# Last norm moved behind the next output, weight sums moved to VectorE, and gate staging regrouped in a one-core encoder block

## The chip, the cores and the metric

The kernel runs on one core of a Trainium2 chip. The metric is the device time of one execution in microseconds (us). The core's engines are named as the profile names them: PE (TensorE matmul) and PEld (its weight loads), DVE (VectorE), ACT (ScalarE), POOL (GpSimd) and SP (SyncE, which here only issues DMAs). Each engine works through its own queue in order and waits on semaphores set by the others.

## The reference

One layer over 16 meta tokens and 1024 frames of width 1024, all in float32:

```python
h = concat([meta, x])                                # 1040 x 1024
xn = rms_norm(h, g0);  proj = xn @ w_in              # q, k, v, forget gate, two output gates
o_a = forgetting_attention(q_a, k_a, v_a, log_f)     # 8 heads of 64
o_b = stick_breaking_attention(q_b, k_b, v_b)        # 8 heads of 64
mixed = (sigmoid(g_a) * (o_a @ w_o_fox) + sigmoid(g_b) * (o_b @ w_o_sb)) @ w_out
h = h + rms_norm(mixed, g1)
u = causal_depthwise_conv(rms_norm(h, g2) @ w_up, conv_w, conv_b)   # 3 taps, 2 x 2816 channels
u_gate, u_val = split(u, 2)
ffn = (gelu(u_gate) * u_val) @ w_down                # 2816 -> 1024
h = h + rms_norm(ffn, g3);  return h[:, 16:]
```

## The kernel before

Features lie on the 128 partitions and tokens along the free axis. Every float32 product is made from two halves, a rounded high part and a rest ("hi" and "lo", of type fp32r): weight hi times input hi, weight hi times input lo, weight lo times input hi. A weight block is loaded into a raw buffer (`load_w`, tag `wraw`, three buffers), ACT casts the high half, and another engine subtracts it for the low half.

The order of instructions on each engine is not written out. A scheduler goes through the program with a timeline simulation of its own and puts instructions that are ready on the engines by priority, which is program order unless `tc.high_priority` lifts it. A tile with a `tag` takes one of the tag's `bufs` buffers and waits until the tile that held it has been read for the last time.

The stages in order:

- Heads. Sixteen heads of attention, with the projections and the gate products (`gate(x)`, 16 of them; the last seven come after the heads in program order) as further work for PE. A gate product is made in three token pieces (`PCS`: 246, 390 and 390 columns after the first 14 are dropped), scaled on DVE into a staging tile `gst` (L485) and stored to memory `gd` (L486). The tag `gst` has two buffers for all three pieces.
- Output projection (L567 on). For each of eight feature blocks `o`, `load_w(wo[o])` with the low half subtracted on POOL, the products `y`, and the gates, loaded again from `gd`.
- Merge and up-projection of the first value and gate blocks as plain products (`plain_tile`), interleaved with the second norm. Their results `us` (value and gate half in one tile) are stored to `ud` for a later convolution.
- Strassen stage. `strassen(lf, js, nxt)` makes one pair of up-projection blocks (gate, value) from seven products instead of eight for each of the token blocks `js`. `Left` prepares the left operands of the following pair in four parts: `first` loads the weights and forms the four sums s1 to s4 (L760 to L763, on POOL, 128x512 each, into `sA` and `sB`), `second`, `third` and `fourth` cast and split. The seven products end in copies on ACT (`keep`, L793 and L824) and adds on DVE (L797), both lifted by priority. At its end `conv_gate` does the convolution of value and then gate (`c`: one ACT instruction L720, two on DVE L722 each), GELU on ACT (L725), their product on DVE (L726), and the store to `gdr`. In six of the pairs `late_conv` does the same for a `us` stored before. The tile `c` has two buffers for the gate and one for the value.
- Down-projection. The 512-token blocks t = 0 and t = 1 are taken one after the other. `hidden(t, k)` loads a block of the hidden layer again (tag `graw`, three buffers) and splits it. `down(t, [o])` makes output block `o` from 22 inputs in pieces of 8, 7 and 7 (`CK`), 66 matmuls of 512 columns, with weights through `wraw`; then ACT squares the result (`fs`, L935), DVE sums the squares (`sas`, L936), and ACT stores the scaled result in `acc` (L937). `last_norm(t, c0, c1)` forms the norm (L133 on: two small groups of matmuls, a square root on ACT, and DVE in between), multiplies `acc` by it (L950), adds the residual `hr` loaded from `hd` (L951; `hr` takes `wraw` buffers) and stores the output (L952). For t = 1 the weights of the last two output blocks are kept (`kept`, loads named `wr_k`, all twelve after output 2), because these outputs are made in two halves of 256 tokens at the end, where the first half's norm runs beside the second half's products.

The lines at the end of the down-projection that set the order:

```python
        last_norm(0, 0, NB)
        for o in range(KT - 2):
            down(1, [o])
            if o == 2:
                ...
        for c0 in (0, 256):
            for o in (KT - 2, KT - 1):
                down(1, [o], c0, c0 + 256, kept)
                if c0 and o == KT - 2:
                    last_norm(1, 0, 256)
        last_norm(1, 256, NB)
```

Of the kernel before, what the change touches and what calls it, by code (L numbers as in the profile page):

```python
# [8 lines left out]
F32 = mybir.dt.float32  # L9
# [40 lines left out]
def block_kernel(ctx, tc, xa, xb, wqk, wv, wf, bfg, wg, wo, wout, wup, wdn, gains, conv, cst, out):  # L50
# [114 lines left out]
    with ExitStack() as pa:  # L165
# [309 lines left out]
        def gate(x):  # L475
            i = x // 2 + 8 * (x % 2)
            hi, lo = load_w(wg[i], KT * P, f"g{i}")
            for k, (n0, n1) in enumerate(PCS):
                m0 = max(n0, A0)
                w = n1 - m0  # L480
                ps = pl.tile([P, 512], F32, tag="lin", name=f"pg{i}{k}")
                products(ps[:, :w], hi, lo, xs[k], 0, KT, m0 - n0, n1 - n0)
                st = xp.tile([P, 390], F32, tag="gst", bufs=2, name=f"gst{i}{k}")
                with tc.high_priority(offset=200):
                    nc.vector.tensor_tensor(st[:, :w], ps[:, :w], rs1[:, m0:n1], op=ALU.mult)  # L485
                nc.sync.dma_start(gd[i][:, m0 - A0 : n1 - A0], st[:, :w])  # L486

# [49 lines left out]
    with ExitStack() as pb1:  # L537
# [29 lines left out]
        for o in range(KT):  # L567
            hi, lo = load_w(wo[o], KT * P, f"o{o}")
            if o > 1:
# [131 lines left out]
    def plain_tile(k, j, s, us, eng=None):  # L701

        wt = load_w(wup[2 * k + s], KT * P, f"u{k}{j}{s}", eng or nc.vector)
        r = right[j]
        for c in range(2):
            ps = bank(f"pu{k}{j}{s}{c}")
            mm3(ps, wt, [r[f"b{kh + 1}{c + 1}"] for kh in range(2)])
            nc.scalar.copy(us[:, s, c, :], ps)

    def u_tile(k, j):  # L710
        return cvp.tile([P, 2, 2, QW], F32, tag="us", bufs=2, name=f"us{k}{j}")

    def conv_gate(k, j, us):
        cv = []
        for s in (1, 0):
            x = 2 * k + s
            c = cvp.tile([P, 2, 256], F32, tag=f"c{s}", bufs=2 - s, name=f"c{x}{j}")
            cv.append(c)
            u = us[:, s]
            nc.scalar.activation(c, u[:, :, 2:QW], AF.Identity, bias=cb[:, x, 3:4], scale=cb[:, x, 2:3])  # L720
            for tap in (1, 0):
                nc.vector.scalar_tensor_tensor(c, u[:, :, tap : tap + 256], cb[:, x, tap : tap + 1], c,  # L722
                                               op0=ALU.mult, op1=ALU.add)
        v, g = cv
        nc.scalar.activation(g, g, AF.Gelu_apprx_tanh)  # L725
        nc.vector.tensor_tensor(g, g, v, op=ALU.mult)  # L726
        nc.sync.dma_start(gdr[k][:, j * NB : (j + 1) * NB], g.rearrange("p h t -> p (h t)"))

    def late_conv(k):
        us = u_tile(k, 0)  # L730
        nc.sync.dma_start(us, ud[k])
        conv_gate(k, 0, us)

    class Left:
# [13 lines left out]
        def first(self):  # L748
# [10 lines left out]
            s2, s4, s3, s1 = self.sA[:, 0:512], self.sA[:, 512:1024], self.sB[:, 0:512], self.sB[:, 512:1024]  # L759
            nc.gpsimd.tensor_tensor(s1, a21, self.a22, op=ALU.add)  # L760
            nc.gpsimd.tensor_tensor(s2, s1, a11, op=ALU.subtract)
            nc.gpsimd.tensor_tensor(s4, a12, s2, op=ALU.subtract)
            nc.gpsimd.tensor_tensor(s3, a11, a21, op=ALU.subtract)  # L763

# [9 lines left out]
    def strassen(lf, js, nxt, kept_order=None):  # L774
# [27 lines left out]
        for j in js:  # L802
            r = psR.tile([P, 512], F32, tag="R", name=f"R{k}{j}")[:, :QW]
            product("a12", "b21", j, r, True)
            add(us[j][:, 0, 0, :], r, kept["p1", j])
        if nxt:
# [8 lines left out]
        for j in js:  # L815
            product("s1", "t1", j, A[j])
            keep(j, "v")
            add(us[j][:, 1, 1, :], B[j], kept["v", j])
        if nxt:
            nxt.second()  # L820
        for j in js:
            product("s4", "b22", j, A[j])
            with tc.high_priority(offset=400):
                nc.scalar.copy(us[j][:, 0, 1, :], A[j])  # L824
        if nxt:
            nxt.third()
        for j in js:
            product("a22", "t4", j, B[j])
            add(us[j][:, 1, 0, :], B[j], kept["u2", j])
        if nxt:  # L830
            nxt.fourth()
        for j in js:
            conv_gate(k, j, us[j])

# [6 lines left out]
    for x in range(2 * NPL):  # L841
        k, s = x // 2, x % 2
        if s == 0:
            us = u_tile(k, 0)
        plain_tile(k, 0, s, us)
        if s:
            nc.sync.dma_start(ud[k], us)
        go(2 if x in (0, 1, 2, 3) else 1)
# [51 lines left out]
    with ExitStack() as pd:  # L900
# [15 lines left out]
        def down(t, os, c0=0, c1=NB, kept=None):  # L916

            w = c1 - c0
            if os[0] == 0:
                sas.append(dpb.tile([P, NB], F32, tag="sas", name=f"sas{t}"))  # L920
            pss = [psD.tile([P, 512], F32, tag="dn", name=f"pd{t}{o}{c0}")[:, :w] for o in os]
# [8 lines left out]
            for o, ps in zip(os, pss):  # L930
                if o == 0:
                    nc.scalar.activation(sa, ps, AF.Square)
                else:
                    s2 = dpb.tile([P, 512], F32, tag="fs", name=f"fs{t}{o}{c0}")[:, :w]
                    nc.scalar.activation(s2, ps, AF.Square)  # L935
# [3 lines left out]
        def last_norm(t, c0, c1):  # L939
# [4 lines left out]
            for o in range(0, KT, st):  # L944
                hr = wp.tile([P, st, w], F32, tag="wraw", bufs=3, name=f"hr{t}{c0}{o}")
                for c in range(c0, c1, 256):
                    nc.sync.dma_start(hr[:, :, c - c0 : c - c0 + 256], hd[2 * t + c // 256][:, o : o + st, :])
                for q in range(0, st, 2):
                    a = acc[:, o + q : o + q + 2, :]
                    nc.vector.tensor_tensor(a, a, rs.to_broadcast([P, 2, w]), op=ALU.mult)  # L950
                    (nc.gpsimd if o < 4 else nc.vector).tensor_tensor(a, a, hr[:, q : q + 2, :], op=ALU.add)  # L951
                    (nc.sync if q else nc.scalar).dma_start(  # L952
                        out[o + q : o + q + 2, :, t * NB + c0 : t * NB + c1].rearrange("k p t -> p k t"), a)
# [9 lines left out]
        for k in range(11, NK):  # L963
            hidden(1, k)
        last_norm(0, 0, NB)
        kept = {KT - 2: [], KT - 1: []}
        KC = [(k, min(k + 4, NK)) for k in range(0, NK, 4)]
        for o in range(KT - 2):
            down(1, [o])
            if o == 2:  # L970
                end = None
                n = 0
                for j, (k0, k1) in enumerate(KC):
                    for x in kept:
                        c = (k1 - k0) * P
                        if c == 512 or end is None:
                            end = slot(dpa if n < 5 else dpb, f"k{n}")
                            n += 1
                            wt = [e[:, :c] for e in end]
                        else:  # L980
                            wt = [e[:, c : 2 * c] for e in end]
                        if c == 512:
                            end = None
                        load_w(wdn[x][:, k0 * P : k1 * P], c, f"k{x}{j}", nc.vector, wt)
                        kept[x].append(wt)
        for c0 in (0, 256):
# [76 lines left out]
```

## Time and profile before

| What | Value |
|---|---|
| Median of 3 runs | 1746.5 us (1746.47 to 1746.73) |
| The profiled execution's own time | 1743.7 us |
| Its span in the trace | 1741.7 us |
| PE busy | 1652.4 us, 95% of the span |
| DVE busy | 1145.1 us, 66% |
| ACT busy | 821.5 us, 47% |
| POOL busy | 578.3 us, 33% |

The span is the time between the first and the last instruction of the profiled execution; the execution's own time lies around it. In the windows of the profile each engine has its busy us and, in brackets, the number of its instructions, in the order PE, PEld, DVE, ACT, POOL, followed by the granted clock of PE (1.00 is full), the share of DMA time and GB/s. A timeline's row gives start, duration, engine, line, operation and tiles, and in brackets at the end what the engine waited for. In a row of grouped instructions the last bar is followed by the idle time ahead of them and its releaser.

### The profile page before, as it was taken

What the parts mean: (1) busy time and instruction counts of PE and PEld (TensorE: products, weight loads), DVE (VectorE), ACT (ScalarE), POOL (GpSimd) and SP (SyncE); (2) the same over time, 40 slices, a digit from 0 to 9 for tenths busy, and PEclk for the clock granted to TensorE, in tenths of its full rate; (3) what the DMA queues carried; (4) which work ended last, traced back from release to release, by engine and by line L of the source; (5) the groups of instructions that cost most, each with busy time, mean ns of one, the idle gap of its engine ahead of it and who ended that gap; (6) DMA issues with size and microseconds to landing.
All of it is one profiled execution on the core that took longest, in us unless ns stands there. A gap on an engine that the chain in (4) does not pass through costs nothing.

```text
span 1741.7 us, 29748 instructions
## 1 busy us (share of the span) xinstructions
PE 1652.4 (95%) x11592; PEld 1586.6 (91%) x11592; DVE 1145.1 (66%) x1881; ACT 821.5 (47%) x1702; POOL 578.3 (33%) x402
## 2 busy tenths in 40 slices
PE   7999999999989899989999999998999999996897
PEld 7899999999989899989999999998999998884687
DVE  8656566665879887745436885999887877333322
ACT  4345445544556565444345554555454556332321
POOL 3456556565445564314302013222232300001001
PEclk9999999999999899999999999999999999997899
DMA  4222221211111012265343542333213238444421
GB/s 166 71 64 63 63 61 59 61 57 52 38 43 41 27 50 63 63 189 159 96 146 125 180 148 71 110 110 116 97 68 103 68 130 251 134 141 149 144 81 61
DMA packets 78237, 170.59 MB, mean 98 GB/s; under 512 B 10224, under 2 KB 37360, under 8 KB 78096
## 3 DMA queue, kind: packets, MB, share of 16 engines
q1 hardware_dynamic: 75920, 165.54, 30.5%
q10 hardware_dynamic: 2176, 3.15, 0.5%
q8 instruction: 91, 1.49, 0.4%
q14 instruction: 50, 0.41, 0.1%
HBM read 126.43 MB, written 35.77 MB: 93 GB/s over the span
## 4 chain that ended last, share of the span: by engine, by line
PE 73%; DVE 12%; DMA 6%; ACT 4%; issue 3%; POOL 0%; DVEq 0%; SPq 0%; ACTq 0%; POOLq 0%
PE pd L913 12%; PE pg L118 9%; PE pq L118 9%; PE A L786 7%; PE pm L611 5%; PE y L118 5%; PE pv L118 5%; PE pu L611 4%; DVE c L722 4%; PE po L431 4%; PE B L786 3%; PE tr L421 3%; PE R L786 2%; PE s L349 2%; PE s L348 2%
## 5 line engine op out<-in xcount | busy, mean ns | idle before, releaser
L913 PE MATMUL pd<-g,wh_d 128*128 128x512 f32 x616 | 194.8, 397 | 23.4 <-ACT wh_d L106 21.9
L722 DVE SCALAR_TENSOR_TENSOR c<-us,cb,c 128x512 f32<-128x512 f32 x176 | 161.6, 932 | 21.5 <-ACT c L720 20.1
L913 PEld LDWEIGHTS pd<-g,wh_d 128*128 128x128 f32 x616 | 117.3, 191 | 51.8 <-ACT wh_d L106 23.9
L393 POOL TENSOR_SCALAR pr<-pr,mx 128x144 f32<-128x144 f32 (+3 forms) x64 | 114.9, 1801 | 102.6 <-DVE mx L392 63.5
L913 PE MATMUL pd<-g,wl_d 128*128 128x512 f32 x308 | 122.4, 397 | 0.4 <-DVE wl_d L92 0.3
L426 DVE TENSOR_TENSOR pt<-tr,pt 128x512 fp32r<-128x512 f32 (+1 forms) x160 | 98.2, 632 | 36.9 <-ACT pt L425 34.3
L401 POOL TENSOR_TENSOR pr<-pr,kp 128x143 f32<-128x143 f32 (+3 forms) x64 | 80.5, 1258 | 121.6 <-DVE kp L398 69.6
L951 POOL TENSOR_TENSOR acc<-acc,hr 128x512 f32<-128x512 f32 (+1 forms) x6 | 9.7, 1639 | 332.7 <-DVE acc L950 332.7
L92 DVE TENSOR_TENSOR wl_d<-wr_d,wh_d 128x896 fp32r<-128x896 f32 (+1 forms) x42 | 47.7, 1137 | 109.8 <-ACT wh_d L106 108.6
L760 POOL TENSOR_TENSOR sB<-wu 128x512 f32<-128x512 f32 x20 | 26.3, 1317 | 279.2 <-DVE s3wlo L92 196.1
L431 PE MATMUL po<-pt,vv 128*128 128x256 f32 (+1 forms) x640 | 110.1, 282 | 7.7 <-DVE pt L426 5.9
L431 PEld LDWEIGHTS po<-pt,vv 128*128 128x128 f32 x640 | 94.6, 190 | 9.7 <-DVE pt L426 6.8
L425 ACT CAST pt<-tr 128x512 fp32r<-128x512 f32 (+1 forms) x160 | 83.0, 545 | 35.6 <-PE tr L421 33.9
L106 ACT CAST wh_d<-wr_d 128x896 fp32r<-128x896 f32 (+1 forms) x42 | 41.1, 979 | 121.2 <-PE pd L913 100.4
L720 ACT ACTIVATE c<-us,cb 128x512 f32<-128x512 f32 x88 | 71.2, 816 | 52.3 <-DVE c L726 23.6
L386 ACT ACTIVATE pr<-s,mx 128x144 f32<-128x144 f32 (+6 forms) x112 | 59.8, 540 | 75.9 <-DVE mx L384 60.3
L421 PE MATMUL tr<-cs,pr 128*128 128x128 f32 x576 | 91.2, 275 | 0.0
L398 DVE TENSOR_TENSOR_SCAN kp<-kp 128x16 f32<-128x16 f32 (+3 forms) x64 | 89.1, 1394 | 0.4
L118 PE MATMUL pg<-xh,wh_g 128*128 128x390 f32 (+1 forms) x384 | 76.0, 331 | 4.9 <-DVE gst L485 4.9
L348 PE MATMUL s<-k,q 128*128 128x264 f32 (+9 forms) x240 | 80.1, 338 | 0.0
L118 PE MATMUL pq<-xl,wh_qk 128*128 128x390 f32 (+1 forms) x384 | 78.7, 329 | 0.0
L118 PE MATMUL pq<-xh,wh_qk 128*128 128x390 f32 (+1 forms) x384 | 77.7, 329 | 0.0
(288 smaller groups left out, 4745.8 us busy)
## 6 DMA issues: line engine op xcount, KB each, us to landing
wu<-in_wup SPq DMA_DIRECT2D x40, 512.0 KB
wr_d<-in_wdn SPq DMA_DIRECT2D x28, 448.0 KB
gdr<-c SPq DMA_DIRECT2D x44, 256.0 KB
gr<-gdr SPq DMA_DIRECT2D x44, 256.0 KB
gs<-gd SPq DMA_DIRECT2D x16, 513.0 KB
wr_qk<-in_wqk SPq DMA_DIRECT2D x16, 512.0 KB
wr_g<-in_wg SPq DMA_DIRECT2D x16, 512.0 KB
wr_wo<-in_wout SPq DMA_DIRECT2D x16, 512.0 KB
```

The lines of the kernel that those rows point to most:

```text
L118: marks["mm"] = nc.tensor.matmul(ps, w[:, k * P : (k + 1) * P], x[:, k - k0, n0:n1], start=(k == k0 and s == 0), stop=(k == k1 - 1 and s = ...
L348: nc.tensor.matmul(ps[:tn, :n], q2[:, t0 : t0 + tn], k1[:, s0:s1], start=True, stop=False)
L393: nc.gpsimd.tensor_scalar(pr[:, :w], pr[:, :w], z, None, op0=ALU.mult)
L398: nc.vector.tensor_tensor_scan(r, r, r, kp[:, w - P : w - P + 1], op0=ALU.mult, op1=ALU.bypass)
L421: nc.tensor.transpose(tr[:, x * P : (x + 1) * P], prs[tb][:, NM + j * P : NM + (j + 1) * P], ident)
L425: nc.scalar.copy(pt[:, 0, :n], tr[:, :n])
L426: nc.vector.tensor_tensor(pt[:, 1, :n], tr[:, :n], f(pt[:, 0, :n]), op=ALU.subtract)
L431: nc.tensor.matmul(po[:, o0:256], vj, pt[:, s, 256 * j : min(256 * j + 256, n)], start=False, stop=(last and j == 1 and s == 1))
L611: nc.tensor.matmul(ps, (hi, hi, lo)[s][:, c : c + P], xs[kh][s == 1][:, k, :], start=(s == 0 and kh == 0 and k == 0), stop=(s == 2 and kh ...
L722: nc.vector.scalar_tensor_tensor(c, u[:, :, tap : tap + 256], cb[:, x, tap : tap + 1], c, op0=ALU.mult, op1=ALU.add)
L786: nc.tensor.matmul(ps, w[:, (k0 + i) * P : (k0 + i + 1) * P], x[:, i, :], start=(first and s == 0 and i == 0), stop=(s == 2 and i == 3), s ...
L913: nc.tensor.matmul(ps, a[:, (k - k0) * P : (k - k0 + 1) * P], x[:, c0:c1], start=(k == 0 and s == 0), stop=(k == NK - 1 and s == 2))
```

## The change

- Gate staging: pieces 0 and 1 go to one tile of 636 columns with one store, piece 2 to a tile of 390 columns; each tile has its own tag and one buffer.
- Output projection: the low halves of `wo` are subtracted on DVE.
- `us` becomes two tiles, one for each half; `ud` is stored and loaded in two parts. The convolution of a half is a function of its own, `half_conv`. In `strassen` the gate half is convolved ahead of the last product (a22 with t4); in the other places the gate comes first and then the value.
- The sums s1 to s4 are made on DVE.
- The norm of block 0 comes after output 0 of block 1. Its residual tiles are eight tiles of 512 columns with tag `graw`, each loaded in two parts, and all its adds are on DVE. The squares `fs` take `graw` buffers too, and `sas` has a buffer for each block. Of the stores of `out` only one kind stays on the ACT queue (second half of block 1, even pairs); the others go through SP.
- The kept weights are loaded two at a time after each of block 1's first six outputs.

```diff
@@ gate
-                st = xp.tile([P, 390], F32, tag="gst", bufs=2, name=f"gst{i}{k}")
+                if k != 1:
+                    st = xp.tile([P, PCS[1][1] - A0 if k == 0 else L - PCS[1][1]], F32, tag=f"gst{k}", name=f"gst{i}{k}")
+                    a0 = m0
                 with tc.high_priority(offset=200):
-                    nc.vector.tensor_tensor(st[:, :w], ps[:, :w], rs1[:, m0:n1], op=ALU.mult)
-                nc.sync.dma_start(gd[i][:, m0 - A0 : n1 - A0], st[:, :w])
+                    nc.vector.tensor_tensor(st[:, m0 - a0 : n1 - a0], ps[:, :w], rs1[:, m0:n1], op=ALU.mult)
+                if k:
+                    nc.sync.dma_start(gd[i][:, a0 - A0 : n1 - A0], st)
@@ output projection
-            hi, lo = load_w(wo[o], KT * P, f"o{o}")
+            hi, lo = load_w(wo[o], KT * P, f"o{o}", nc.vector)
@@ us, conv_gate
-        return cvp.tile([P, 2, 2, QW], F32, tag="us", bufs=2, name=f"us{k}{j}")
...
+        return [cvp.tile([P, 2, QW], F32, tag=f"us{s}", bufs=2, name=f"us{s}{k}{j}") for s in range(2)]
+
+    def half_conv(k, j, s, u):
+        x = 2 * k + s
+        c = cvp.tile([P, 2, 256], F32, tag=f"c{s}", bufs=2 - s, name=f"c{x}{j}")
+        nc.scalar.activation(c, u[:, :, 2:QW], AF.Identity, bias=cb[:, x, 3:4], scale=cb[:, x, 2:3])
+        for tap in (1, 0):
+            nc.vector.scalar_tensor_tensor(c, u[:, :, tap : tap + 256], cb[:, x, tap : tap + 1], c,
+                                           op0=ALU.mult, op1=ALU.add)
+        if s == 0:
+            nc.scalar.activation(c, c, AF.Gelu_apprx_tanh)
+        return c
+
+    def conv_gate(k, j, us, g=None):
+        g = half_conv(k, j, 0, us[0]) if g is None else g
+        v = half_conv(k, j, 1, us[1])
         nc.vector.tensor_tensor(g, g, v, op=ALU.mult)
         nc.sync.dma_start(gdr[k][:, j * NB : (j + 1) * NB], g.rearrange("p h t -> p (h t)"))
@@ late_conv
-        nc.sync.dma_start(us, ud[k])
+        for s in range(2):
+            nc.sync.dma_start(us[s], ud[k][:, s])
@@ Left.first
-            nc.gpsimd.tensor_tensor(s1, a21, self.a22, op=ALU.add)
-            nc.gpsimd.tensor_tensor(s2, s1, a11, op=ALU.subtract)
-            nc.gpsimd.tensor_tensor(s4, a12, s2, op=ALU.subtract)
-            nc.gpsimd.tensor_tensor(s3, a11, a21, op=ALU.subtract)
+            nc.vector.tensor_tensor(s1, a21, self.a22, op=ALU.add)
+            nc.vector.tensor_tensor(s2, s1, a11, op=ALU.subtract)
+            nc.vector.tensor_tensor(s4, a12, s2, op=ALU.subtract)
+            nc.vector.tensor_tensor(s3, a11, a21, op=ALU.subtract)
@@ strassen
         if nxt:
             nxt.third()
+        gs = {j: half_conv(k, j, 0, us[j][0]) for j in js}
         for j in js:
             product("a22", "t4", j, B[j])
-            add(us[j][:, 1, 0, :], B[j], kept["u2", j])
+            add(us[j][1][:, 0, :], B[j], kept["u2", j])
         if nxt:
             nxt.fourth()
         for j in js:
-            conv_gate(k, j, us[j])
+            conv_gate(k, j, us[j], gs[j])
@@ down
-                    s2 = dpb.tile([P, 512], F32, tag="fs", name=f"fs{t}{o}{c0}")[:, :w]
+                    s2 = dpa.tile([P, 512], F32, tag="graw", bufs=3, name=f"fs{t}{o}{c0}")[:, :w]
@@ last_norm
-                hr = wp.tile([P, st, w], F32, tag="wraw", bufs=3, name=f"hr{t}{c0}{o}")
-                for c in range(c0, c1, 256):
-                    nc.sync.dma_start(hr[:, :, c - c0 : c - c0 + 256], hd[2 * t + c // 256][:, o : o + st, :])
+                if w == NB:
+                    hr = [dpa.tile([P, NB], F32, tag="graw", bufs=3, name=f"hr{t}{o + i}") for i in range(st)]
+                else:
+                    hr = wp.tile([P, st, w], F32, tag="wraw", bufs=3, name=f"hr{t}{c0}{o}")
+                    nc.sync.dma_start(hr, hd[2 * t + c0 // 256][:, o : o + st, :])
                 for q in range(0, st, 2):
                     a = acc[:, o + q : o + q + 2, :]
                     nc.vector.tensor_tensor(a, a, rs.to_broadcast([P, 2, w]), op=ALU.mult)
-                    (nc.gpsimd if o < 4 else nc.vector).tensor_tensor(a, a, hr[:, q : q + 2, :], op=ALU.add)
-                    (nc.sync if q else nc.scalar).dma_start(
+                    if w == NB:
+                        for i in range(2):
+                            for c in range(2):
+                                nc.sync.dma_start(hr[i][:, 256 * c : 256 * (c + 1)], hd[2 * t + c][:, o + i, :])
+                            nc.vector.tensor_tensor(a[:, i, :], a[:, i, :], hr[i], op=ALU.add)
+                    else:
+                        (nc.gpsimd if o < 4 else nc.vector).tensor_tensor(a, a, hr[:, q : q + 2, :], op=ALU.add)
+                    (nc.scalar if c1 == NB and c0 and not q else nc.sync).dma_start(
                         out[o + q : o + q + 2, :, t * NB + c0 : t * NB + c1].rearrange("k p t -> p k t"), a)
@@ order of the down-projection
-        last_norm(0, 0, NB)
...
+        def keep_w(j, x):
...
+            load_w(wdn[x][:, k0 * P : k1 * P], c, f"k{x}{j}", nc.vector, wt)
+            kept[x].append(wt)
+
         for o in range(KT - 2):
             down(1, [o])
-            if o == 2:
...
+            if o == 0:
+                last_norm(0, 0, NB)
+            for x in kept:
+                keep_w(o, x)
```

More of the change, by code (lines that the diff above doesn't have):

```diff
@@ L707, in plain_tile @@
             mm3(ps, wt, [r[f"b{kh + 1}{c + 1}"] for kh in range(2)])
-            nc.scalar.copy(us[:, s, c, :], ps)
+            nc.scalar.copy(us[s][:, c, :], ps)
     def u_tile(k, j):
-        return cvp.tile([P, 2, 2, QW], F32, tag="us", bufs=2, name=f"us{k}{j}")
[L713 to L725, printed above, removed]
+        return [cvp.tile([P, 2, QW], F32, tag=f"us{s}", bufs=2, name=f"us{s}{k}{j}") for s in range(2)]
[12 more added lines that the diff above has]
+        v = half_conv(k, j, 1, us[1])
         nc.vector.tensor_tensor(g, g, v, op=ALU.mult)
@@ L804, in strassen @@
             product("a12", "b21", j, r, True)
-            add(us[j][:, 0, 0, :], r, kept["p1", j])
+            add(us[j][0][:, 0, :], r, kept["p1", j])
         if nxt:
@@ L817, in strassen @@
             keep(j, "v")
-            add(us[j][:, 1, 1, :], B[j], kept["v", j])
+            add(us[j][1][:, 1, :], B[j], kept["v", j])
         if nxt:
@@ L823, in strassen @@
             with tc.high_priority(offset=400):
-                nc.scalar.copy(us[j][:, 0, 1, :], A[j])
+                nc.scalar.copy(us[j][0][:, 1, :], A[j])
         if nxt:
             nxt.third()
+        gs = {j: half_conv(k, j, 0, us[j][0]) for j in js}
         for j in js:
             product("a22", "t4", j, B[j])
-            add(us[j][:, 1, 0, :], B[j], kept["u2", j])
+            add(us[j][1][:, 0, :], B[j], kept["u2", j])
         if nxt:
@@ L846, in block_kernel @@
         if s:
-            nc.sync.dma_start(ud[k], us)
+            for u in range(2):
+                nc.sync.dma_start(ud[k][:, u], us[u])
         go(2 if x in (0, 1, 2, 3) else 1)
@@ L919, in down @@
             if os[0] == 0:
-                sas.append(dpb.tile([P, NB], F32, tag="sas", name=f"sas{t}"))
+                sas.append(dpb.tile([P, NB], F32, name=f"sas{t}"))
             pss = [psD.tile([P, 512], F32, tag="dn", name=f"pd{t}{o}{c0}")[:, :w] for o in os]
@@ L964, in block_kernel @@
             hidden(1, k)
-        last_norm(0, 0, NB)
         kept = {KT - 2: [], KT - 1: []}
         KC = [(k, min(k + 4, NK)) for k in range(0, NK, 4)]
+        end = None
+        def keep_w(j, x):
+            nonlocal end
+            k0, k1 = KC[j]
+            c = (k1 - k0) * P
+            if c == 512 or end is None:
+                n = 2 * j + x % 2
+                end = slot(dpa if n < 5 else dpb, f"k{n}")
+                wt = [e[:, :c] for e in end]
+            else:
+                wt = [e[:, c : 2 * c] for e in end]
+            if c == 512:
+                end = None
+            load_w(wdn[x][:, k0 * P : k1 * P], c, f"k{x}{j}", nc.vector, wt)
+            kept[x].append(wt)
         for o in range(KT - 2):
             down(1, [o])
-            if o == 2:
[L971 to L985, printed above, removed]
+            if o == 0:
+                last_norm(0, 0, NB)
+            for x in kept:
+                keep_w(o, x)
         for c0 in (0, 256):
```

## The prediction

> **What bounds the kernel now.** I read the page's busy table first, then the windows stage by stage, then the waits of PE, and at each wait the chain or the timelines.
>
> ```profile
> span 1741.7 us, 29748 instructions
> PE 1652.4 (95%) x11592; PEld 1586.6 (91%) x11592; DVE 1145.1 (66%) x1881; ACT 821.5 (47%) x1702; POOL 578.3 (33%) x402
> 1100.00:1200.00 100.00, 94.43 (x771) 93.18 (x772) 93.96 (x116) 58.03 (x98) 29.91 (x20) 1.00 0.31 100
> 1200.00:1400.00 200.00, 191.53 (x1562) 188.93 (x1561) 164.75 (x201) 103.38 (x177) 64.64 (x44) 1.00 0.27 90
> 1500.00:1550.00 50.00, 50.00 (x221) 41.09 (x220) 13.14 (x15) 13.46 (x18) 0.00 (x0) 1.00 0.33 96
> 1573.74:1593.43 19.69, 3.12 (x10) 1.47 (x11) 10.00 (x10) 3.77 (x5) 4.66 (x2) 0.56 0.43 141
> 1573.74:1693.50 119.76, 95.01 (x392) 75.11 (x392) 40.49 (x43) 32.41 (x44) 4.66 (x2) 0.87 0.42 131
> ```
>
> PE (the first busy column of a window; then PEld, DVE, ACT, POOL, granted clock) is the bound nearly everywhere, so the change can win only where PE stands still. Three places belong to it. The Strassen stage (1100 to 1400) loses 5.57 + 8.47 = 14.0 us of PE, with DVE at 94% in its first third. The hole after 1573.74 leaves PE 16.6 us without work. And the second block's first six outputs of the down-projection, 1573.74 to 1693.50, are 6 x 66 = 396 matmuls that take 119.76 us; at the undisturbed pace of the 1500 to 1550 row, 50.00 / 221 = 0.2262 us each, they are 89.6 us.
>
> ```profile
> PE A L786 <- ACT v L793: 4.7, 4, 1.4
> PE A L786 <- DVE a11wlo L92: 3.3, 4, 1.1
> PE B L786 <- ACT s3whi L743: 2.8, 4, 0.7
> PE B L786 <- DVE us L797: 2.5, 2, 1.9
> PE pd L913 <- ACT wh_d L106: 21.9, 2, 13.8
> ```
>
> PE's waits of the two stages (total, times, longest): 13.3 us in the Strassen stage, all on ACT or DVE work that comes late; 21.9 us in the down-projection, two holes. Their chain and the SP timeline:
>
> ```profile
> 1577.51 2.09 PE rr_d L148 x2
> 1584.24 2.58 DVE acc L951
> 1586.84 5.48 DMA out<-acc
> 1592.33 1.05 ACT wh_d L106
> 1565.88 18.44 SPq L947 DMA_DIRECT2D hr<-hd  x4
> 1586.84 31.57 SPq L99 DMA_DIRECT2D wr_d<-in_wdn  x9
> 1623.18 19.70 SPq L99 DMA_DIRECT2D wr_k<-in_wdn  x12
> 1644.14 31.02 SPq L99 DMA_DIRECT2D wr_d<-in_wdn  x9
> ```
>
> First hole: the last norm of block 0 stands ahead of block 1's weights. Its residual tiles `hr` hold the three `wraw` buffers; the first weight load goes out at 1586.84, when the add that reads `hr` ends (1584.24 + 2.58), and PE restarts one load and one cast later. The chain calls that load a store, but the SP row shows `wr_d` issued at that moment. Second hole: twelve loads `wr_k` occupy the same three buffers from 1623.18 and the next `wr_d` waits until 1644.14.
>
> **The change, term by term.** (1) Last norm and kept weights. `hr` moves from `wraw` to `graw`, so no weight load waits for it. The norm comes after block 1's first output, so while it runs three pieces of weights are in or on their way. The kept loads go two per output instead of twelve in a row. Both holes lose their cause. What remains in place: the norm's own matmuls, and DVE work that stands in front of weight splits.
>
> ```profile
> 1721.13 0.50 PE L138 MATMUL rp_d<-cs,sas 128*128 128x1 f32 x4
> 1725.26 0.59 PE L148 MATMUL rr_d<-dg_d,one_sq 128*128 128x256 f32 x2
> L950 DVE TENSOR_TENSOR acc<-acc,rr_d 128x1024 f32<-128x1024 f32 x4 | 4.6, 1217 | 2.2 <-PE rr_d L148 2.2
> L726 DVE TENSOR_TENSOR c<-c,c 128x512 f32<-128x512 f32 x6 | 4.1, 685 | 0.0
> 1593.43:1603.43 10.00, 9.96 (x36) 7.58 (x37) 3.39 (x3) 1.88 (x2) 0.00 (x0) 0.83 0.62 226
> 1649.09:1659.09 10.00, 9.96 (x31) 7.49 (x32) 2.79 (x3) 1.88 (x2) 0.00 (x0) 0.72 0.33 115
> ```
>
> The matmuls cost PE 0.50 plus twice 0.59 for the double width, 1.5 us with rounding. DVE gets four multiplications (4.6 us) and, now all on it, eight adds of 512 columns at 0.69 (the L726 row has that shape): 10.1 us. A weight piece keeps PE busy 24 x 0.2262 = 5.4 us, and its successor's cast and split need 1.05 + 1.23 (the chain's 1.05, and 1.2 as in the multiplication's row), so some 3 us of slack per piece meets single instructions of 0.7 to 1.2 us. Where an add waits for its `hr`, the split queued behind it on DVE waits too; SP has sixteen `hr` loads of 128 KB instead of eight of 256 KB, and the four stores move from the ACT queue to SP, where each waits for an add and holds whatever is behind it. I put 1.5 us on that, between 0 (all within the slack) and 13.7 (priced as a rival below). The extra 2 x 256 KB per output lie under 15 us of matmuls. The squares that now share `graw` hold a buffer only until DVE has added them; an output's PSUM has four banks, so a late square delays no matmul by itself. Sum: 119.76 - 89.6 - 1.5 - 1.5 = 27.2 us saved. About 5 us of it is the slow clock after each hole, not the holes: 36 and 31 matmuls in 10 us where 44 fit.
>
> (2) Strassen stage. Four sums per weight block move from POOL to DVE, 80 in all.
>
> ```profile
> L722 DVE SCALAR_TENSOR_TENSOR c<-us,cb,c 128x512 f32<-128x512 f32 x176 | 161.6, 932 | 21.5 <-ACT c L720 20.1
> L722 DVE SCALAR_TENSOR_TENSOR c<-us,cb,c 128x512 f32<-128x512 f32 x22 | 16.4, 748 | 2.0 <-ACT c L720 2.0
> L92 DVE TENSOR_TENSOR a22ul<-wu,a22uh 128x512 fp32r<-128x512 f32 x19 | 29.1, 1534 | 0.0
> L92 DVE TENSOR_TENSOR a22ul<-wu,a22uh 128x512 fp32r<-128x512 f32 x1 | 0.7, 690 | 0.0
> L760 POOL TENSOR_TENSOR sB<-wu 128x512 f32<-128x512 f32 x16 | 21.1, 1318 | 174.7 <-DVE s3wlo L92 174.7
> 1146.51 3.42 DVE L722 SCALAR_TENSOR_TENSOR c<-us,cb,c 128x512 f32<-128x512 f32 x2
> 1146.33 1.32 POOL L760 TENSOR_TENSOR sB<-wu 128x512 f32<-128x512 f32 x1 [13.89 <-DVE s3wlo L92]
> 1147.61 1.77 POOL L763 TENSOR_TENSOR sB<-wu,wu 128x512 f32<-128x512 f32 x1
> 1143.22 1.05 ACT L743 CAST s3whi<-sB 128x1024 fp32r<-128x1024 f32 x1
> 1164.75 1.05 ACT L743 CAST s3whi<-sB 128x1024 fp32r<-128x1024 f32 x1
> ```
>
> The same DVE instruction takes 748 ns in the window 1400 to 1450, where POOL has nothing, and 932 on average over the stage; a22ul takes 690 alone and 1534 in the stage. In the timeline two L722 that stand beside POOL's sums take 3.42 us together. So POOL's sums already cost DVE 176 x 0.184 + 19 x 0.844 = 48 us. On DVE itself the 80 sums are 80 x 0.69 = 55 us. DVE's load thus stays as it is, within 7 us over 350 us. What changes is lateness: a 1.7 us stall in front of an urgent add goes, and a 0.69 us sum that has some 15 us until its cast (L763 writes sB until 1149.38, and its cast runs at 1164.75) comes instead. The gate half, convolved before the last product and gate first in the late blocks, lets its GELU on ACT follow two DVE steps instead of four, which is where "A <- ACT v" comes from: the copy that frees bank A is queued on ACT behind a GELU that waits for DVE. The split `us` adds six loads and six stores on SP, hidden as the old ones were. I take the 2.5 us of "us" fully and half of the 10.8 us of the other three waits: 2.5 + 5.4 = 7.9 us saved. Bounds: all 13.3; and below nothing, 9 us lost, if the L722 stay as slow as they are and the sums come on top in the six blocks with late convolutions: one takes 21.5 us (1143.22 to 1164.75) and 0.94 x 21.5 = 20.2 of DVE; with 4 x 0.69 more that is 23.0, 1.5 longer, six times.
>
> The Trainium skill, "SBUF — State Buffer", section "Who interferes with whom", says a DVE instruction with two SBUF inputs and a GpSimd instruction that reads SBUF exclude each other for the whole instruction. The rows agree that both get longer, but not that all of POOL's time is lost to DVE. By that rule of the Trainium skill the return would be POOL's whole busy time in the stage, 29.9 + 64.6 = 95 us of 1100 to 1400, and the 55 us of sums would be more than paid; by the rows it is the 48 us above.
>
> (3) Gate staging and output projection. The two stores per gate replace three; pieces 0 and 1 share one buffer, so the next gate's first product waits for a store issued after piece 1 rather than for one two pieces back. In the head loop these stores have tens of us. In the last gates they have not:
>
> ```profile
> 744.00:784.00 40.00, 33.98 (x218) 33.37 (x217) 20.12 (x40) 17.04 (x37) 8.38 (x5) 0.91 0.76 207
> PE pg L118 <- DVE gst L485: 4.9, 1, 4.9
> 762.49 1.01 SPq L486 DMA_DIRECT2D gd<-gst  x2
> ```
>
> Both stores left only at 762.49, behind loads on SP; with one store of 318 KB in the place of the two the wait lasts about as long. I take 0, between 6.0 us gained (all of PE's idle time in that window) and 5 lost (the wait once more, for the larger store). The eight low halves of `wo` cost DVE 1.2 us each instead of POOL's time, beside a DVE that is half idle: 0; without that cover 8 x 1.2 = 10 us.
>
> (4) Tail: block 1's first half stores all go through SP, so ACT no longer issues a store ahead of its last square:
>
> ```profile
> 1729.83 0.38 ACTq L952
> ```
>
> 0.4 us saved, all of this row, since SP has nothing else there that the end waits for.
>
> Sum: 27.2 + 7.9 + 0 + 0.4 = 35.5 us. The profiled execution took 1743.7 us (span 1741.7), so 1708.2; the median of the runs shown lies 2.8 above it: 1711.
>
> **The rivals.** A. The Strassen stage gives nothing back, since DVE's load is unchanged and other late instructions replace those: 27.6 us saved, 1719. Against it stands that POOL's sums now hit urgent instructions at random.
> B. The first hole moves rather than goes: the norm's eight `hr` tiles pass three `graw` buffers in three rounds of 5.5 us (the load at 1586.84), with 10.1 us of DVE in order, 26.6 us, under one output's cover of 66 x 0.2262 = 14.9 us; 11.7 us exposed plus 2 of slow clock, 13.7. In the place of the 1.5 allowed, of term 1 then 15.0 remain, with the rest 23.3: 1723.
> C. DVE is freed by the whole of POOL's busy time and all 13.3 us come back, and the gate stage gains a little: 27.2 + 13.3 + 0.4 and up to 6.0, 41 to 47 saved, 1700 to 1706. The 932 against 748 speaks for less. (By the rule of the Trainium skill's SBUF page named above it would come out so.)
> D. Slower than before: DVE becomes the bound of the Strassen stage. If L722 is slow for another reason than POOL and each sum takes as long as a22ul does there (1.53), 80 sums add 122 us to a DVE that has only 41 us of room in 1100 to 1400 (300 - 93.96 - 164.75): some 80 us lost against 27.6 saved, 1799. It decides against the change above (41 + 27) / 80 = 0.86 us per sum with L722 unchanged. The 690 and 748 rows, both with POOL idle, speak against it.
> E. The change doesn't do what it says: a scheduled order that again puts `wr_d` behind the norm's work and the kept loads. Then only term 2 is left, or nothing: about 1739 to 1746.
>
> **How the numbers follow.** My forecast 0.55, A 0.20, B 0.09, C 0.09, D 0.04, E 0.03. Changes below about 0.2% (3.5 us) can hardly be told from none here; the forecast and A to C are all beyond that, and E is split. Faster 0.94, same 0.02, slower 0.04. The range reaches from 1701, inside C, to 1726, just above B.
>
> **What would show it.** Term 1: no PE wait on `wh_d` over 2 us after the first block's end, a granted clock of 1.00 through it, and 396 matmuls in about 93 us. Term 2: POOL empty in the Strassen stage, L722 at about 750 ns throughout, DVE's busy share there within a few per cent of before, and PE's waits there near 5 us. Term 3: PE's idle time of 744 to 784 still near 6 us. The forecast falls if the waits on `wh_d` come back behind `hr` or behind the stores on SP, if L722 stays near 930, or if PE waits in the Strassen stage for sums queued on DVE.

## The result, and the profile after

| | Time, us | Ratio to before, 95% interval |
|---|---|---|
| Before | 1746.5 | |
| Changed | 1705.6 | 0.9764 (0.9745 to 0.9783) |
| Changed, measured a second time | 1706.0 | 0.9765 (0.9752 to 0.9778) |

The change saves 41 us where 35.5 were forecast; 1705.6 lies inside the range of 1701 to 1726. One of the changed kernel's four executions took 3219.85 us and one of the ten of experiment e3 2019.0; the medians count them, the ratios leave them out.

The page of the changed kernel, its busy table:

```profile
span 1704.2 us, 29666 instructions
PE 1648.1 (97%) x11592; PEld 1585.0 (93%) x11592; DVE 1139.8 (67%) x1975; ACT 821.0 (48%) x1702; POOL 440.1 (26%) x312
```

PE has lost 4 us of busy time and 33 us of idle time; DVE has 94 instructions more and is busy 5 us less. To see where the time came from, the span is cut at two moments that exist in every trace: the first Strassen product, and the first matmul `pd` of the down-projection. The stage between them in the kernel before, in the changed one and, for later use, with the sums alone (e2) and without the early gate half (e10):

```profile
1043.51:1450.17 406.66, 392.62 (x3219) 388.56 (x3217) 333.04 (x420) 221.61 (x378) 110.73 (x76) 1.00 0.31 103
1044.32:1437.99 393.67, 390.67 (x3219) 389.14 (x3217) 323.36 (x495) 223.29 (x378) 0.00 (x0) 1.00 0.31 104
1045.97:1435.74 389.77, 388.09 (x3218) 387.26 (x3217) 323.66 (x495) 223.07 (x378) 0.00 (x0) 1.00 0.32 105
1043.25:1433.11 389.86, 388.14 (x3218) 387.30 (x3217) 323.39 (x494) 222.93 (x378) 0.00 (x0) 1.00 0.32 105
```

The first number after the window is its length. The stage falls from 406.7 to 393.7 us. Before it, 0.8 us were lost (1043.51 against 1044.32). After it, the down-projection with its tail takes 1704.2 - 1438.0 = 266.2 us against 1741.7 - 1450.2 = 291.5. So 13.0 + 25.3 - 0.8 = 37.5 us, the difference of the two spans. (The medians differ by more, 41 us, because the profiled execution of the kernel before lay 2.8 us under its median.)

PE's waits in the changed kernel's Strassen stage (the first four rows), in its down-projection (the next four; two more on the hidden layer `g` add 1.0 us) and at the last gates:

```profile
PE A L791 <- ACT us L829: 1.1, 1, 1.1
PE A L791 <- DVE s2ul L92: 0.8, 1, 0.8
PE B L791 <- ACT s3whi L748: 0.7, 1, 0.7
PE A L791 <- ACT p L798: 0.5, 1, 0.5
PE pd L920 <- DVE wl_d L92: 1.5, 4, 0.7
PE pd L920 <- ACT wh_d L106: 1.5, 1, 1.5
PE rr_d L148 <- DVE dg_d L144: 1.1, 1, 1.1
PE rp_d L138 <- DVE sas L943: 0.9, 1, 0.9
PE pg L118 <- DVE gst L487: 3.1, 1, 3.1
```

The fourteen small waits of the prediction's rows (13.3 us) have become four (3.1 us), and the two holes of 21.9 us one wait of 1.5 and four of 1.5 together. The DVE rows of 1060 to 1460 say why the first went:

```profile
L721 DVE SCALAR_TENSOR_TENSOR c<-us,cb,c 128x512 f32<-128x512 f32 x176 | 128.7, 746 | 22.0 <-ACT c L719 21.2
L92 DVE TENSOR_TENSOR a22ul<-wu,a22uh 128x512 fp32r<-128x512 f32 x19 | 13.0, 683 | 0.2 <-ACT a22uh L748 0.2
L765 DVE TENSOR_TENSOR sB<-wu 128x512 f32<-128x512 f32 x18 | 12.3, 682 | 0.0
```

The convolution's DVE instruction takes 746 ns in place of 932, a22ul 683 in place of 1534, and a sum costs 0.68 us.

### The profile page after: what moved, and what is told of

Read it like the earlier page. It is cut to its first block, busy times and chain, and to the rows that moved or that the text cites. A ratio compares the mean times of both kernels' runs of the same rounds, so it can differ in the third digit from the quotient of the medians.

```text
span 1704.2 us, 29666 instructions
## 1 busy us (share of the span) xinstructions
PE 1648.1 (97%) x11592; PEld 1585.0 (93%) x11592; DVE 1139.8 (67%) x1975; ACT 821.0 (48%) x1702; POOL 440.1 (26%) x312
## 4 chain that ended last, share of the span: by engine, by line
PE 84%; DVE 6%; DMA 4%; ACT 2%; issue 2%; SPq 0%; POOL 0%; DVEq 0%; ACTq 0%; POOLq 0%
PE A L791 12%; PE pd L920 11%; PE pg L118 9%; PE pq L118 9%; PE B L791 6%; PE pm L614 5%; PE y L118 5%; PE pv L118 5%; PE pu L614 4%; PE po L431 4%; PE tr L421 3%; PE R L791 3%; PE s L349 2%; PE s L348 2%; DMA gr<-gdr 2%
## 5 line engine op out<-in xcount | busy, mean ns | idle before, releaser
L966 POOL TENSOR_TENSOR acc<-acc,hr 128x512 f32<-128x512 f32 x4 | 5.0, 1282 | 737.2 <-DVE acc L959 737.2
L721 DVE SCALAR_TENSOR_TENSOR c<-us,cb,c 128x512 f32<-128x512 f32 x176 | 128.7, 746 | 22.0 <-ACT c L719 21.2
L401 POOL TENSOR_TENSOR pr<-pr,kp 128x143 f32<-128x143 f32 (+3 forms) x64 | 80.4, 1258 | 121.0 <-DVE kp L398 69.7
L118 PE MATMUL pq<-xh,wl_qk 128*128 128x390 f32 (+1 forms) x384 | 76.7, 325 | 0.0
```

The lines of the kernel that those rows point to most:

```text
L118: marks["mm"] = nc.tensor.matmul(ps, w[:, k * P : (k + 1) * P], x[:, k - k0, n0:n1], start=(k == k0 and s == 0), stop=(k == k1 - 1 and s = ...
```

## The experiments

Each kernel was run beside the kernel before on the same chip; the median of the latter was 1745.8 us for e1 to e4, 1746.4 for e5 to e8 and 1746.5 for the others, and "less" below is counted from it. The ratio is not the quotient of the two medians and differs from it by up to 0.001. The last two columns are read from one trace each: from the first Strassen product to the first `pd`, and from there to the end of the span.

| Kernel | Median, us | Ratio, 95% interval | Strassen stage | Down-projection |
|---|---|---|---|---|
| before | 1746.5 | | 406.7 | 291.5 |
| changed | 1705.6 | 0.9764 (0.9745 to 0.9783) | 393.7 | 266.2 |
| e1 down-projection alone | 1721.3 | 0.9856 (0.9841 to 0.9870) | 407.4 | 268.8 |
| e2 sums alone | 1728.8 | 0.9895 (0.9879 to 0.9912) | 389.8 | 293.0 |
| e3 gate half alone | 1742.9 | 0.9979 (0.9967 to 0.9991) | 403.1 | 291.8 |
| e4 gate staging and wo alone | 1744.1 | 0.9987 (0.9975 to 0.9998) | 406.9 | 291.2 |
| e5 changed, POOL reading | 1730.3 | 0.9911 (0.9888 to 0.9935) | 419.0 | 265.3 |
| e6 changed, POOL filling | 1705.8 | 0.9770 (0.9748 to 0.9792) | 393.7 | 267.0 |
| e7 changed, norm first | 1704.5 | 0.9768 (0.9740 to 0.9796) | 392.5 | 266.2 |
| e8 changed, kept at once | 1716.8 | 0.9828 (0.9806 to 0.9851) | 392.5 | 278.4 |
| changed again | 1706.0 | 0.9765 (0.9752 to 0.9778) | 392.4 | 269.5 |
| e9 changed, last residual in graw | 1703.8 | 0.9756 (0.9743 to 0.9770) | 392.5 | 266.7 |
| e10 changed without early gate half | 1702.7 | 0.9751 (0.9737 to 0.9766) | 389.9 | 269.3 |
| e11 e10 with e9 | 1702.6 | 0.9752 (0.9739 to 0.9765) | 390.1 | 268.2 |

**Each part alone: e1 to e4.** The edits are the parts of the diff above, applied singly to the kernel before: the down-projection (`down`, `last_norm`, `keep_w`), the four lines of `Left.first`, the two tiles of `us` with `half_conv`, and `gate` with `wo`.

> The kernel before with only the changes of the down-projection (norm of block 0 behind output 0 of block 1, its residual tiles and the squares in graw, kept weights two per output). Theory: both holes of PE go by themselves, without help from the other parts: about 25.5 us faster than before (1721), no wait on wh_d over 2 us. Rival (the parts need each other: without the shorter Strassen stage the holes reappear elsewhere): under 20 us faster.

e1 takes 1721.3 us, 24.4 less than before. The holes go without help from the other parts; what is left of the waits on weights is one of 3.2 us (so not quite the "under 2 us" expected) and four small ones:

```profile
PE pd L913 <- ACT wh_d L106: 3.2, 1, 3.2
PE pd L913 <- DVE wl_d L92: 1.6, 4, 0.7
```

> The kernel before with only the sums s1 to s4 on DVE. Theory (POOL's sums block DVE, and the late DVE instructions make PE wait): L722 falls from 932 to about 750 ns, PE's waits of the Strassen stage from 13.5 to about 5 us, 8 to 10 us faster. Rival 1 (the order of the gate half brings the Strassen gain): L722 falls but the waits stay, 0 to 3 us faster. Rival 2 (DVE gets busier): slower by up to 9 us.

e2 takes 1728.8 us, 16.9 less: more than the theory expected, and as much as its Strassen stage became shorter (406.7 to 389.8). The waits of PE in the stage sum to 1.7 us, and L722 is at 746:

```profile
PE B L786 <- ACT s3whi L743: 0.7, 1, 0.7
PE A L786 <- ACT us L824: 0.5, 1, 0.5
PE A L786 <- ACT p L793: 0.3, 1, 0.3
PE A L786 <- ACT s2uh L743: 0.2, 1, 0.2
L722 DVE SCALAR_TENSOR_TENSOR c<-us,cb,c 128x512 f32<-128x512 f32 x176 | 129.3, 746 | 30.3 <-ACT c L720 29.2
```

Both rivals fall: the order of the gate half is not needed for the gain, and DVE does not become the bound. One thing is not separated here: four sums take 4 x 0.68 = 2.7 us on DVE and took 5.9 on POOL, so they are also ready earlier. e5 below shows what slower DVE instructions do by themselves.

> The kernel before with only the two tiles of us and the gate half convolved ahead of the last product and first elsewhere; sums still on POOL. Theory (sums matter most): 2 to 4 us faster, L722 still near 930 ns, the waits for the copy of bank A (4.7 us before) gone. Rival 1: 10 to 13 us faster, the whole Strassen gain.

e3 takes 1742.9 us, 2.8 less (3.7 by the ratio), as expected of a side effect. Its rows show the mechanism that the prediction gave it, and its limit: the waits for the copy of bank A went from 4.7 to 0.7 us, but those for the cast of s3 rose from 2.8 to 6.0, and L718 (the convolution's line there) is still at 899.

```profile
PE B L788 <- ACT s3whi L745: 6.0, 4, 3.9
PE A L788 <- ACT v L795: 0.7, 1, 0.7
L718 DVE SCALAR_TENSOR_TENSOR c<-us,cb,c 128x512 f32<-128x512 f32 x176 | 156.0, 899 | 20.0 <-ACT c L716 19.0
```

> The kernel before with only the two stores per gate and the low halves of wo on DVE. Theory: PE's idle time around the last gates goes from 6.0 to about 3.5 us, as in the changed kernel, 1 to 3 us faster or lost in the noise. Rival (it costs: the start of the output projection came 1.2 us later in the changed kernel): 1 us slower.

e4 takes 1744.1 us, 1.7 less, with an interval that just excludes no change. Its one wait for `gst` is 1.0 us, against 4.9 before and 3.1 in the changed kernel:

```profile
PE pg L118 <- DVE gst L487: 1.0, 1, 1.0
```

The four parts alone save 24.4 + 16.9 + 2.8 + 1.7 = 45.8 us, the whole 41. So they do not quite add up, at the edge of what the intervals resolve; e10 below looks at one of them.

**What POOL does to DVE: e5 and e6.** Useless work for POOL beside the sums on DVE. e5 subtracts weights into a scratch tile, e6 fills the scratch tile:

```diff
+            jk = upB.tile([P, 256], F32, tag="jk", name=f"jk{self.k}")
+            for x, y in ((a21, self.a22), (a11, a21), (a12, a11), (a21, a12)):      # e5
+                for c in (0, 256):
+                    nc.gpsimd.tensor_tensor(jk, x[:, c : c + 256], y[:, c : c + 256], op=ALU.subtract)
...
+            for v in range(24):                                                    # e6
+                nc.gpsimd.memset(jk, 0.0)
```

> The changed kernel, with useless work on POOL beside the sums on DVE: per weight block eight subtractions of 128x256 from the weights into a scratch tile that nobody reads. Theory (POOL instructions that read SBUF hold up DVE instructions with two SBUF inputs): L721 of the changed kernel rises from 746 to 900 ns or more, PE's waits of the Strassen stage from 3 to over 10 us, 8 us or more slower than the changed kernel. Rival (DVE was slow for another reason, and the gain is the order of work): L721 stays near 746 and the time stays within 2 us.

> The changed kernel, with useless work on POOL that reads nothing: per weight block 24 fills of 128x256 with a constant into the scratch tile. If POOL's reads are what holds DVE up: L721 at 746 to 760 ns and the time of the changed kernel within 2 us. If any work of POOL does: L721 well over 800 ns and slower by several us.

DVE and POOL rows of 1060 to 1460, first e5 (with the two longest rows of PE's waits in its stage), then e6:

```profile
PE B L795 <- DVE us L806: 5.5, 5, 3.0
PE A L795 <- DVE a11wlo L92: 5.1, 3, 1.9
L721 DVE SCALAR_TENSOR_TENSOR c<-us,cb,c 128x512 f32<-128x512 f32 x173 | 143.8, 846 | 19.3 <-ACT c L719 18.4
L768 DVE TENSOR_TENSOR sB<-wu,wu 128x512 f32<-128x512 f32 x18 | 22.0, 1222 | 0.0
L772 POOL TENSOR_TENSOR jk<-wu,wu 128x256 f32<-128x256 f32 x72 | 83.9, 1166 | 5.6
```

```profile
L721 DVE SCALAR_TENSOR_TENSOR c<-us,cb,c 128x512 f32<-128x512 f32 x176 | 128.9, 747 | 22.2 <-ACT c L719 21.3
L771 POOL MEMSET jk<- 128x256 f32 x413 | 129.0, 312 | 23.7
```

With POOL reading, the same DVE instructions are slow again (746 to 846 ns, the sum L768 from 684 to 1222), PE's waits in the stage come back (21.2 us, the longest on the same late DVE work as in the kernel before), and the kernel takes about 24.5 us more than the changed one. L721 rises less than to the 900 ns expected; the slowness now falls on the sums too. With POOL filling for 129 us, longer than it worked in the kernel before, nothing moves: 747 ns and 1705.8 us. So it is POOL's reading that costs DVE, not its being busy. The Trainium skill, "SBUF — State Buffer", section "Who interferes with whom", states just this distinction for a DVE instruction with two SBUF inputs (a GpSimd instruction that reads SBUF against one that only writes it), and the two runs agree.

That the whole of POOL's time is lost to DVE, as rival C had it, the runs do not bear out. In 1060 to 1460 of the kernel before POOL was busy for 105.6 us, and DVE's instructions there were longer than in the changed kernel by 54 us in all (L722 33, a22ul 16, the product L726 4, s2ul 1).

**The two holes apart: e7 and e8.**

```diff
+        last_norm(0, 0, NB)                    # e7: ahead of block 1's first output again
         for o in range(KT - 2):
             down(1, [o])
-            if o == 0:
-                last_norm(0, 0, NB)
...
-            for x in kept:                     # e8: all twelve after output 2 again
-                keep_w(o, x)
+            if o == 2:
+                for j in range(KT - 2):
+                    for x in kept:
+                        keep_w(j, x)
```

> The changed kernel with the norm of block 0 back ahead of block 1's first output; its residual tiles stay in graw and the kept weights stay spread. If the three wraw buffers taken by the residual made the first hole: no hole, within 3 us of the changed kernel. If the place in the order made it (the norm's matmuls, DVE work and stores ahead of the weights): a hole of 8 to 15 us, that much slower than the changed kernel.

e7 takes 1704.5 us, the same as the changed kernel within the interval. SP's rows (first the changed kernel, then e7) show that the scheduler issued the norm in the same place: from the first `pd` (1437.99 and 1432.84) to this first load of `hr` it is 144.0 us in the changed kernel and 143.9 in e7.

```profile
1582.02 2.69 SPq L963 DMA_DIRECT2D hr<-hd  x6
1576.70 2.69 SPq L963 DMA_DIRECT2D hr<-hd  x6
```

So with `hr` in buffers of its own the place of the norm in the program did not matter. Since the order on the engines stayed that of the changed kernel, e7 does not test the old order there. That the three `wraw` buffers made the first hole rests on the chain of the kernel before, where the weight load goes out when the add that reads `hr` ends; a kernel with the norm moved and `hr` left in `wraw` was not tried, nor one with `hr` alone moved.

> The changed kernel with all twelve kept loads after output 2 again. Theory: the second hole comes back, 8 us of PE idle and 2 us of slow clock, 8 to 10 us slower than the changed kernel. Rival (the holes were linked, and with the first gone the weights are far enough ahead): within 2 us.

e8 takes 1716.8 us, 11 more than the changed kernel. The second hole is back, on the same chain: ten of the twelve kept loads in a row from 1603.21, the next weights at 1618.18, and PE without work for 8.7 us.

```profile
PE pd L920 <- ACT wh_d L106: 9.1, 2, 8.7
1603.21 13.89 SPq L99 DMA_DIRECT2D wr_k<-in_wdn  x10
1618.18 30.84 SPq L99 DMA_DIRECT2D wr_d<-in_wdn  x9
```

**Two further steps: e9 to e11**, run side by side with the changed kernel on one chip. e9 takes the last residual tile out of `wraw`; e10 is the changed kernel with the old `u_tile`, `conv_gate`, `late_conv` and without the early `half_conv`; e11 is both.

```diff
-                    hr = wp.tile([P, st, w], F32, tag="wraw", bufs=3, name=f"hr{t}{c0}{o}")
+                    if c0 and o:                                                   # e9
+                        hr = [dpa.tile([P, 2, w], F32, tag="graw", bufs=3, name=f"hr{t}{c0}{o}{q}") for q in range(0, st, 2)]
...
-        gs = {j: half_conv(k, j, 0, us[j][0]) for j in js}                         # e10
```

> The changed kernel once more, to be compared with the next three on the same chip: 1704 to 1707 us, 0.976 of the kernel before.

> The changed kernel with the last residual tile (second half of block 1, features 512 up) in two graw buffers instead of the third round of wraw, so that its load does not wait behind the four stores of out on SP. Theory (the changed kernel's end waits for that load: 5.3 us in its chain): the time from the last matmul to the end falls from 12.2 to about 10.5 us, 1 to 2 us faster than the changed kernel. Rival (the stores set the end anyway): same time.

In the changed kernel the chain ends on the last residual load, which goes out on SP behind the four stores that the change had put there (first fence). e9 and e11 do not bring the load ahead of them: its two halves go out right behind the four stores, 1.4 us after the end of the last product as in the changed kernel (second fence e9, third e11). In e9 the chain still ends on the load; in e11 it goes by the norm's multiplications.

```profile
1693.62 0.49 SPq L956 DMA_DIRECT2D hr<-hd  x1
1693.62 5.30 DMA hr<-hd
1699.02 0.93 DVE acc L966
```

```profile
1688.77 3.27 SPq L974 DMA_DIRECT2D out<-acc  x4
1692.09 1.19 SPq L959 DMA_DIRECT2D hr<-hd  x2
1692.09 4.53 DMA hr<-hd
```

```profile
1687.23 3.29 SPq L970 DMA_DIRECT2D out<-acc  x4
1690.57 1.17 SPq L955 DMA_DIRECT2D hr<-hd  x2
1693.07 2.23 DVE acc L962 x4
```

The last square on ACT by the timeline, first in the changed kernel, then in e11, last in the kernel before (start, length, and in brackets the idle time ahead of it):

```profile
1692.30 0.38 ACT L942 ACTIVATE fs<-pd 128x256 f32<-128x256 f32 x1 [7.82 <-PE pd L920]
```

```profile
1689.24 0.38 ACT L938 ACTIVATE fs<-pd 128x256 f32<-128x256 f32 x1 [7.81 <-PE pd L916]
```

```profile
1730.31 0.38 ACT L935 ACTIVATE fs<-pd 128x256 f32<-128x256 f32 x1 [8.08 <-PE pd L913]
```

The end hardly moves: from the last square on ACT to the end of the span it is 11.9 us in the changed kernel (1692.30 to 1704.2) and 11.7 in e11 (1689.24 to 1700.9). From the end of the last product it is 12.0 us in both traces of the changed kernel and 11.4 in e9, but also 11.4 and 11.5 in e6 and e8, whose end is that of the changed kernel. So no gain of 1 to 2 us is there, and what the load itself costs is not told by these runs, since neither e9 nor e11 moved it ahead of the stores. e9's median is 2.2 us lower than that of the changed kernel beside it; the two intervals overlap.

> The changed kernel without the gate half convolved early (us as one tile, value first, conv_gate at the end as before); sums, gate staging, wo and the down-projection as changed. Theory (with the sums on DVE the early gate half only costs: the kernel with the sums alone had 1.7 us of PE idle in the Strassen stage against 3.0): 2 to 4 us faster than the changed kernel. Rival (it helps by the 2.8 us it gave alone): 2 to 3 us slower.

> Without the early gate half, and the last residual tile in graw: both gains if both theories hold, 3 to 6 us faster than the changed kernel, about 1701 us.

e10 and e11 are the lowest, 1702.7 and 1702.6, 3.3 us under the 1706.0 of the changed kernel beside them; the intervals overlap, so that they are faster is not settled by the times. The stage is clearer: without the early gate half it takes 389.8 to 390.1 us in three traces (e2, e10, e11), with it 392.4 to 393.7 in six that have the sums on DVE and no extra reads on POOL. In the first four rows of waits above, "A <- ACT us" is the copy that ends s4's product, and it is longest with the early gate half (1.1 us, against 0.5 in e2). The waits are only a part of it: PE's busy time in the stage is also longer with the early half (389.4 to 390.7 us, against 388.1 in e2, e10 and e11), and why was not tried. The down-projection of e10 and e11 (269.3 and 268.2 us) lies between the 266.2 and 269.5 of the changed kernel's own two traces, so it tells nothing against them.

## Why the prediction was right, and where its steps were off

In the two traces the forecast of 35.5 us stands against 37.5: term 1 came out 1.7 us lower than forecast, term 2 5.1 us higher. The rest is the later start of the stage and the tail. That the first two partly cancel is luck; the mechanisms of both are in the main as predicted.

- **Term 1, both holes (27.2 us forecast).** Right in mechanism and nearly in size: e1 saves 24.4 us alone. But the window 1573.74 to 1693.50 was taken to hold the 396 matmuls of the first six outputs, and by the trace it holds 375 of 512 columns and 7 of 256; the 396th ends only at 1699.03, with 13 half-width products of the last two outputs put among them. From the end of block 0's last product to the end of the 396th, first before, then changed:

```profile
1573.73:1699.03 125.30, 100.54 (x420) 79.79 (x420) 40.49 (x43) 32.41 (x44) 4.66 (x2) 0.88 0.41 126
1561.45:1661.29 99.84, 97.13 (x419) 77.67 (x419) 47.37 (x59) 36.69 (x54) 0.00 (x0) 0.98 0.57 183
```

The stretch became 25.5 us shorter. At the prediction's pace (0.2262 us, half of that for the half-width ones) its matmuls are 91.0 us, so 34.3 us were lost there before, where the sum had 30.2, and 8.8 remain, where it allowed 3.0: two errors of 4.1 and 5.8 us in opposite directions, and that they nearly cancel is luck. Two of the signs named for this term did not come: the granted clock is 0.98 and not 1.00, and the matmuls take 99.8 us and not about 93.
- **The allowance of 1.5 us** for DVE work in front of weight splits stands against 1.5 us of waits on `wl_d` and 1.5 on `wh_d` in the changed kernel, and 1.6 and 3.2 in e1: too small by a factor of two to three, where the bound of 13.7 was far off. Rival B did not come about; e7, with the norm written first, does not show it either.
- **"The norm comes after block 1's first output, so while it runs three pieces of weights are in or on their way."** The edit that was to bring this about was not needed: with the norm written first the scheduler issues the same order and the time is the same. Whether that order matters on the engines stays open.
- **Term 2, Strassen stage (7.9 us forecast).** Mis-sized: 13.0 us in the changed kernel, 16.9 with the sums alone. Two steps failed. Three of the four waits were halved, with nothing in a row for the half, and next to nothing of them is left (1.7 us of waits in e2, 3.1 in the changed kernel). And only PE's idle time was counted as the price of a wait: the stage before has 392.6 us of busy PE, e2 has 388.1 for the same matmuls. Another 4.5 us thus stood in longer matmuls that count as busy. For this stage the 13.3 us of rival C were the better forecast, though not by its reason: DVE's instructions were 54 us longer beside POOL, not as much as POOL was busy.
- **DVE's load "stays as it is, within 7 us".** Nearly right: 333.0 against 323.4 us of DVE in the stage, 10 less, in spite of 75 more instructions.
- **The gate half, "which is where A <- ACT v comes from".** Right for the kernel before, as e3 shows with 4.7 us falling to 0.7, but it was credited with a part of the gain that the sums alone bring, and with the sums moved it costs 2.4 to 3.9 us of that stage.
- **Term 3 (0).** The stretch of the gates in the changed kernel, against the same window in the prediction (length, then busy time of PE):

```profile
744.00:784.00 40.00, 36.51 (x227) 35.41 (x225) 18.35 (x42) 17.82 (x39) 3.54 (x3) 0.91 0.74 205
```

2.5 us of PE's idle time went there (6.0 to 3.5), where it was expected to stay near 6. How much of that lasts one trace does not tell: the Strassen stage begins between 1040.4 and 1045.8 us in the ten traces with this part of the change and between 1042.8 and 1046.0 in the four without. e4 puts the part at 1.7 us, within the bounds of 6.0 and -5.
- **Term 4 (0.4 saved).** ACT's store was the wait it was said to be: the last square now starts 0.04 us after the last product and not 0.30 (their ends are 1692.26 and 1730.01). But "SP has nothing else there that the end waits for" is wrong: a residual load queues behind the four stores. The time from the last square to the end went from 11.4 us (1730.31 to 1741.7) to 11.9, so the term saved nothing.
- **Rival D.** The point to decide was named as 0.86 us per sum with L722 unchanged; a sum takes 0.68 and L722 falls. e5 shows something of what that rival would have been like: with reads on POOL again (177 us of them in the stage), sums at 0.72 to 1.22 us and L721 at 846 ns, the stage takes 419 us, longer than before the change.

## What to carry to other kernels

When one instruction has two very different durations in one trace, look at what runs beside it: here the sum of the excess over the fast form (48 us by the prediction's rows, 54 as it turned out) was about the price of moving the other engine's work over (55 us), so the move cost nothing and took away the lateness. Price a wait by the stage's length in a run without it, not by its idle time alone, since the matmuls behind a wait may be longer too. When loads share a ring of buffers, look for the tile that holds the ring while it waits for something unrelated: with other buffers for it the place in the program no longer mattered here, and the order written in the program need not be the order that a scheduler issues.

## What the runs showed of the hardware that was not expected

POOL instructions that only write, 413 fills of 312 ns between 1060 and 1460 us, left DVE's two-input instructions at 747 ns. Eight subtractions of half the size per weight block brought them to 846 ns and the four 128x512 sums from 0.68 us to between 0.72 and 1.22. The subtractions seem to pay as well: they took 1166 ns for 256 columns, where a two-input POOL instruction of 271 columns in the heads (L401 of the kernel before) takes 693. But DVE is not shut out for the whole of POOL's busy time: in the kernel before 105.6 us of that went with 54 us of longer DVE instructions.
